# A transformer block on one core: the first row tiles' norm and projection reordered, the last tile's end in whole steps

## The chip, the cores and the metric

One Trainium2 chip, one of its cores. The metric is the device time of one execution in microseconds (us); less is better. Engines are named as in the profile: TensorE (PE; its weight loads are PEld), VectorE (DVE), ScalarE (ACT), GpSimd (POOL), SyncE (SP). SP, ACT and POOL also issue DMA transfers, each from its own instruction stream.

## The reference, cut to what matters

A residual block on x (1 x 1024 x 1024, float32): two parallel token mixers, then a SwiGLU feed-forward, each between two RMS norms.

```
def rmsnorm(x, g):
    y = x * lax.rsqrt(jnp.mean(x * x, axis=-1, keepdims=True) + RMS_EPS)
    return y * g

h = rmsnorm(x, norm_mix_pre[l])              # (1024, 1024)
proj = h @ w_in[l]                           # columns q, k, v, f_logit, g_b, g_c, hc, two gates
logf = log_sigmoid(f_logit + b_f)            # 8 heads
m = (gated short convolution of h, with conv_w) and (forgetting attention on q, k, v, logf), merged
x = x + rmsnorm(m @ w_out[l], norm_mix_post[l])
h = rmsnorm(x, norm_ffn_pre[l])
f = (silu(h @ w_gate) * (h @ w_up)) @ w_down[l]
x = x + rmsnorm(f, norm_ffn_post[l])
```

## The kernel before, in words

Every float32 product is made as three products of split operands: a value a is written as a high half (ScalarE's rounding copy to fp32r) and a low half (VectorE's subtraction of that from a), and a*b is ah*bh + ah*bl + al*bh (`mm3`). Most projections use Strassen's seven products on 512-row blocks, so they need sums of h's blocks (hT12, hT34).

The head, which the change touches, is the first 68 us. x is cut into 8 row tiles of 128 rows (st = 0 to 7), the columns of w_in for v and f_logit (`wv`, 520 columns) into 8 parts of 128 rows (k = 0 to 7). SyncE issues, in this order: row tile 0, the norm's row (4 KB), wv parts 0 to 3, row tile 1, wv parts 4 to 7, row tile 2; the next row tiles follow as their buffers (three) come free. The norm's row is broadcast to 128 partitions by a TensorE matmul with ones (`gmp`), between 10 and 14 turns of the identity (`turns`, transposes whose results nobody reads); ScalarE later copies it to `gm`. For a row tile: ScalarE squares and sums it (`norm_sum`), VectorE and ScalarE make the scale (`rms_scale`), VectorE scales (`norm_rest`, tile hn), TensorE transposes hn in two groups of four (`turn`, tile tp), and ScalarE and VectorE split the transposed tile into halves (hB11 and hB21 for tiles 0 to 3, vf and hB22 for tiles 4 to 7). `split_wv` splits a part of wv into wvh and wvl. `v_tile` then makes v and f_logit of the row tile: for each k and each half of the columns, the three products into `pv`; the result is copied to vs, stored (POOL's queue), and the 8 f columns get the bias bf (`ff`). `rest` copies the transposed tile (tiles 0 to 3, `hraw`) or makes Strassen's sums (tiles 4 to 7). After the last v products (end at 68.04 us) the first two projection heads start: q's first product needs h0 and l0, made early, and k's needs h and l, which ScalarE and VectorE make of a weight tile that waits for the head's memory.

A planner orders instructions per engine by program order and its own time estimates; `strict[0]` names engines whose instructions keep the program's order (`keep_in_program_order`), all engines in the first part of the head. Each engine's instructions run in order; so an instruction that waits holds all behind it.

The end: the feed-forward's down projection makes the last four row tiles' last column half (`product` with `last_parts`): per row tile (sl) 21 products of late operands into one accumulator; then ScalarE squares and sums it, the scale is made, VectorE applies scale and residual (`finish`), SyncE stores. Of the last row tile the last 12 products run as two column halves of 256 (`HALVES`), the square and the multiplication by the norm's row follow each half.

Of the kernel before, what the change touches and what calls it, by code (L numbers as in the profile page):

```python
# [46 lines left out]
def block_kernel(  # L47
# [121 lines left out]
    nc.gpsimd.dma_start(bf, b_f[0].partition_broadcast(P))  # L169

# [72 lines left out]
    xq.append(load_x(1))  # L243
    for _ in range(4):
        load_wv()
# [6 lines left out]
    gm = ax.tile([P, D], F32, name="gm")  # L252


    spin = psa.tile([P, 4, P], F32, tag="mm", name="spin")
    gmp = psa.tile([P, 2, NC], F32, tag="pv", name="gmp", bufs=2)

    def turns(n):
        for _ in range(n):
            nc.tensor.transpose(spin[:, 0, :], ident, ident)  # L260
# [23 lines left out]
    def norm_rest(st, xt, hn, rs):  # L284

        for n in range(2) if st == 0 else (None,):
            c = slice(0, D) if n is None else (n1, n2)[n]
            nc.vector.scalar_tensor_tensor(
                hn[:, c], xt[:, c], rs, gm[:, c] if n is None else gmp[:, n, :],
                op0=ALU.mult, op1=ALU.mult,  # L290
            )
        if st + 3 < ST:
            xq.append(load_x(st + 3))
        return hn
# [5 lines left out]
    hraw = None  # L300

    def turn(st, hn):

        nonlocal hraw
        sl = st % 4
        ss = slice(sl * P, (sl + 1) * P)
        tps = []
        for q in range(2):
            tp = psa.tile([P, 4, P], F32, tag="mm", name="tp")
            for k in range(4):  # L310
                kt = 4 * q + k
                nc.tensor.transpose(tp[:, k, :], hn[:, kt * P : (kt + 1) * P], ident)
            tps.append(tp)
        if st < 4:
            if hraw is None:
                hraw = ah.tile([P, KT, NC], F32, name="hraw")
            ops = []
            for q, hb_ in enumerate((hB11, hB21)):
                hh, hl = (t[:, :, ss] for t in hb_)
                if st == 0:  # L320
                    copy(hh, tps[q])
                    split_wv(q + 2, "h")
                    sub(hl, tps[q], f32(hh))
                    split_wv(q + 2, "l")
                else:
                    split(hh, hl, tps[q])
                ops.append((hh, hl))

            def rest():
                for q in range(2):  # L330
                    copy(hraw[:, 4 * q : 4 * q + 4, ss], tps[q])

# [27 lines left out]

    def v_tile(st, ops):
        pv = psa.tile([P, 2, NC], F32, tag="pv", name="pv", bufs=2)
# [10 lines left out]
        vs = av.tile([P, VF + 8], F32, tag="vs", name="vs", bufs=2)[:, :VF]  # L373
        copy(vs.rearrange("p (n c) -> p n c", n=2), pv[:, :, :HV])
        nc.gpsimd.dma_start(v_dram[st * P : (st + 1) * P, :], vs[:, :AW])
        add(ff[:, st, :], vs[:, AW:VF], bf)

    xt0, hn0, ssq0 = norm_sum(0)
    rs0 = rms_scale(ssq0)
    for k in range(2):  # L380
        split_wv(k, "h")
    norm_rest(0, xt0, hn0, rs0)
    for k in range(2):
        split_wv(k, "l")
    cur = turn(0, hn0)
    split_wv(4)
    one = norm_sum(1)
    split_wv(5)
    for n in range(2):
        copy(gm[:, n * NC : (n + 1) * NC], gmp[:, n, :])  # L390
    rs1 = rms_scale(one[2])
    split_wv(6)
    hn = norm_rest(1, *one[:2], rs1)
    split_wv(7)
    sub(mask, tri, ident)
    nc.vector.tensor_scalar(mask, mask, BIG, None, op0=ALU.mult)
    strict[0] = ("vector", "scalar")
    for st in range(ST):
# [3 lines left out]
        if st + 2 < ST:  # L402
            hn = norm(st + 2)
        if st + 3 == ST:
# [182 lines left out]
    nc.sync.dma_start(cw, conv_w[0].rearrange("t (c p) -> p t c", p=P))  # L587

# [1169 lines left out]
    def down(acc, ops, k, sl, start, stop, first, cols=slice(0, NC)):  # L1758
# [4 lines left out]
            acc[sl][:, cols], (ah[:, k, ss], al[:, k, ss]), (bh[:, k, cols], bl[:, k, cols]),  # L1763
# [3 lines left out]
    def product(acc, first, done, tail=1, between=None, parts=None):  # L1767
# [13 lines left out]
        steps_ = [(g, ops, k) for g, ops in late for k in range(min(2, NK - 2 * g))]  # L1781
# [143 lines left out]
```

## Time and profile before

| | |
|---|---|
| median of 3 runs | 1330.12 us (1329.48 to 1330.79) |
| the profiled execution | 1330.96 us, span 1329.0 us |
| TensorE matmul busy | 1315.5 us (99%), 6717 instructions |
| TensorE weight load | 1091.8 us (82%) |
| VectorE | 966.7 us (73%) |
| ScalarE | 558.0 us (42%) |
| mean granted TensorE clock | 0.999 |

How to read it: times are microseconds from the start of the span. A busy share is an average over stages with different limits; the timeline shows an instruction's start, its duration, and in brackets the idle time of its engine just before it with what ended it. "x8" is a run of eight like instructions merged to one row, whose second number is then their total. The granted clock is a share of TensorE's full speed.

### The profile page before, as it was taken

Reading aid. Unit: us, or ns where it says so; the run is one execution under the profiler, and the core shown is the slowest. Engines: PE = TensorE matmul, PEld = TensorE weight load, DVE = VectorE, ACT = ScalarE, POOL = GpSimd, SP = SyncE. Lnnn points to the kernel's source line nnn. Section 1 sums busy time; section 2 is a strip of 40 time slices with the busy share of each in tenths; the row PEclk is TensorE's granted clock in tenths of the full one; section 3 lists DMA queues with packets and bytes.
Section 4 is the critical chain, followed back from the end, with each engine's and each line's share of the span. In section 5 each row is a group of like instructions: output and inputs, shape, how many; then the busy total and the mean of one; then the engine's idle time right before and its main releaser. Section 6 shows DMA issues by size and latency. Waiting matters only on the chain.

```text
span 1329.0 us, 18042 instructions
## 1 busy us (share of the span) xinstructions
PE 1315.5 (99%) x6717; PEld 1091.8 (82%) x6717; DVE 966.7 (73%) x1532; ACT 558.0 (42%) x898; POOL 143.1 (11%) x272
## 2 busy tenths in 40 slices
PE   9999999999999999999999999999999999999997
PEld 7988888888888888888878888888888888888886
DVE  6974678765656767686699688997767776676685
ACT  6642222233345766514578332322322234444452
POOL 0011000011112212010012112121001110000000
PEclk9999999999999999999999999999999999999999
DMA  5334544455536544476166545553233328876541
GB/s 192 120 119 135 152 110 128 128 166 145 172 111 206 160 136 158 138 237 225 65 216 207 160 157 183 182 191 103 74 109 106 117 102 283 310 255 194 157 165 63
DMA packets 189097, 210.48 MB, mean 158 GB/s; under 512 B 11457, under 2 KB 137473, under 8 KB 189010
## 3 DMA queue, kind: packets, MB, share of 16 engines
q1 hardware_dynamic: 155586, 146.12, 35.5%
q0 software_dynamic: 16528, 54.84, 11.2%
q10 hardware_dynamic: 16896, 8.39, 2.1%
q8 instruction: 52, 0.85, 0.3%
q14 instruction: 35, 0.29, 0.1%
HBM read 150.78 MB, written 58.52 MB: 157 GB/s over the span
## 4 chain that ended last, share of the span: by engine, by line
PE 79%; issue 14%; DVE 2%; ACT 2%; DMA 1%; POOL 1%; DVEq 0%; SPq 0%; POOLq 0%; ACTq 0%
PE b L76 40%; PE pd L76 16%; PE pba L76 3%; PE pbb L76 3%; PE pv L76 3%; PE tps L76 3%; PE po L76 3%; PE p L76 2%; PE sp L76 2%; PE ma L76 1%; PE q L76 1%; DMA raw<-in_w_gate_up_dram 1%; PE mb L76 1%; PE tp L76 1%; POOL qk_dram L76 1%
## 5 line engine op out<-in xcount | busy, mean ns | idle before, releaser
L76 PE MATMUL b<-x,hi 128*128 128x512 f32 x1088 | 335.7, 389 | 0.1
L76 PEld LDWEIGHTS b<-x,hi 128*128 128x128 f32 x1088 | 203.9, 188 | 43.0 <-ACT c L76 0.5
L76 PE MATMUL b<-x,lo 128*128 128x512 f32 x544 | 211.8, 389 | 0.0
L76 DVE TENSOR_TENSOR c<-c,b 128x512 f32<-128x512 f32 x193 | 131.5, 682 | 58.8 <-PE b L76 51.4
L76 DVE TENSOR_TENSOR lo<-raw,hi 128x1024 fp32r<-128x1024 f32 x92 | 110.8, 1204 | 73.5 <-PE b L76 65.7
L76 ACT ACTIVATE hi<-raw 128x1024 fp32r<-128x1024 f32 (+1 forms) x99 | 100.6, 1018 | 96.8 <-PE b L76 50.3
L76 PEld LDWEIGHTS b<-x,lo 128*128 128x128 f32 x544 | 102.1, 188 | 21.4
L76 ACT ACTIVATE hi<-sx 128x1024 fp32r<-128x1024 f32 (+1 forms) x43 | 44.8, 1043 | 147.4 <-PE b L76 140.5
L76 ACT ACTIVATE sgf<-c 128x512 f32<-128x512 f32 x31 | 19.6, 633 | 133.2 <-DVE c L76 114.0
L76 DVE TENSOR_TENSOR lo<-sx,hi 128x1024 fp32r<-128x1024 f32 (+1 forms) x43 | 51.5, 1198 | 27.9 <-PE b L76 26.7
L76 DVE TENSOR_TENSOR sx<-raw 128x512 f32<-128x512 f32 x78 | 53.6, 687 | 19.9 <-DMA raw<-in_w_in_dram 10.4
L76 PE MATMUL pd<-hi,lo 128*128 128x512 f32 (+1 forms) x163 | 62.8, 385 | 0.0
L76 PE MATMUL pd<-hi 128*128 128x512 f32 (+1 forms) x163 | 62.4, 386 | 0.0
L76 PE MATMUL pd<-ghi 128*128 128x512 f32 (+1 forms) x149 | 57.9, 389 | 1.1 <-DVE um L76 1.1
L76 PE MATMUL pd<-glo,ghi 128*128 128x512 f32 (+1 forms) x149 | 57.8, 388 | 0.0
L76 PE MATMUL pd<-ghi,glo 128*128 128x512 f32 (+1 forms) x149 | 57.8, 388 | 0.0
L76 PE MATMUL b<-hT34h,hi 128*128 128x512 f32 x136 | 53.2, 391 | 0.8 <-DVE c L76 0.8
L76 PE MATMUL b<-hT34h,lo 128*128 128x512 f32 x136 | 52.9, 389 | 0.0
L76 PE MATMUL b<-hT34l,hi 128*128 128x512 f32 x136 | 52.9, 389 | 0.0
L76 PE MATMUL b<-hT12h,hi 128*128 128x512 f32 x136 | 52.9, 389 | 0.0
L76 PE MATMUL b<-hT12l,hi 128*128 128x512 f32 x136 | 52.9, 389 | 0.0
L76 PE MATMUL b<-hT12h,lo 128*128 128x512 f32 x136 | 52.9, 389 | 0.0
(427 smaller groups left out, 3050.3 us busy)
## 6 DMA issues: line engine op xcount, KB each, us to landing
raw<-in_w_gate_up_dram SPq DMA_DIRECT2D x55, 512.0 KB, 3.8
raw<-in_w_in_dram SPq DMA_DIRECT2D x35, 512.0 KB, 4.9
a_dramS<-um POOLq DMA_DIRECT2D x44, 256.0 KB, 3.2
a_dramA<-um POOLq DMA_DIRECT2D x33, 256.0 KB, 2.7
sg<-sg_dram SPq DMA_DIRECT2D x32, 256.0 KB, 4.0
x<-wo_dram SPq DMA_DIRECT2D x16, 512.0 KB, 7.4
graw<-a_dramS SPq DMA_DIRECT2D x14, 512.0 KB, 3.6
sg_dram<-c POOLq DMA_DIRECT2D x24, 256.0 KB, 3.6
```

The lines of the kernel that those rows point to most:

```text
L76: ins = getattr(self.engine, name)(*args, **kw)
```

## The change

Head: the norm row is loaded to 128 partitions by a DMA on ScalarE's queue (`gm`), no matmul, no copy; all 26 turns run ahead. wv's odd parts are issued by ScalarE, the even ones by SyncE. `rms_scale` is cut in two functions, hn of tiles 0 and 1 is scaled in two halves. wv's high halves 0 to 2 are made ahead of tile 0's copies, the others behind tile 1's square; low halves 3 to 7 follow tile 1's norm. The products of tiles 0 and 1 are no longer `mm3` per k but sorted: high-high, low-high and high-low apart, with the last high-low ones (k = 6, 7 of tile 0, 4 to 7 of tile 1) behind tile 2's transposes. All engines keep program order up to there. bf, the mask and conv_w are loaded or made later. End: the last row tile takes the same whole steps as the others.

```
@@ head
-    nc.gpsimd.dma_start(bf, b_f[0].partition_broadcast(P))
...
     def rms_scale(ssq, rest=None, tile_=st_tile, w=1):
-        va, sq, r0 = (tile_(n, w) for n in ("va", "sq", "r0"))
+        return rms_finish(*rms_root(ssq, rest, tile_, w), tile_, w)
+
+    def rms_root(ssq, rest=None, tile_=st_tile, w=1):
+        va, sq = (tile_(n, w) for n in ("va", "sq"))
...
+        return va, sq
+
+    def rms_finish(va, sq, tile_=st_tile, w=1):
+        r0 = tile_("r0", w)
         nc.vector.reciprocal(r0, sq)
...
-    def load_wv():
+    def load_wv(engine):
...
-        nc.sync.dma_start(wr, win[k * P : (k + 1) * P, C_V : C_V + VF])
+        engine.dma_start(wr, win[k * P : (k + 1) * P, C_V : C_V + VF])
...
+    gm = ax.tile([P, D], F32, name="gm")
     xq = deque([load_x(0)])
-    grow = ap.tile([P, D], F32, tag="hn", name="grow", bufs=2)[0:1, :]
-    nc.sync.dma_start(grow, norm_mix_pre)
-    for _ in range(4):
-        load_wv()
+    nc.scalar.dma_start(gm, norm_mix_pre[0].partition_broadcast(P))
+    for k in range(3):
+        load_wv((nc.sync, nc.scalar)[k % 2])
     xq.append(load_x(1))
-    for _ in range(4):
-        load_wv()
+    for k in range(3, KT):
+        load_wv((nc.sync, nc.scalar)[k % 2])
     xq.append(load_x(2))
     warm = st_tile("warm")
     nc.scalar.activation(warm, ones[:, 0:1], AF.Sqrt)
...
-    turns(10)
-    for n in range(2):
-        nc.tensor.matmul(
-            gmp[:, n, :], ones[0:1, :], grow[:, n * NC : (n + 1) * NC], start=True, stop=True
-        )
-    turns(14)
+    for _ in range(26):
+        nc.tensor.transpose(spin[:, 0, :], ident, ident)
...
-        for n in range(2) if st == 0 else (None,):
...
+        for c in (n1, n2) if st < 2 else (slice(0, D),):
             nc.vector.scalar_tensor_tensor(
...
+                hn[:, c], xt[:, c], rs, gm[:, c], op0=ALU.mult, op1=ALU.mult
...
+    def turned(hn, q):
+        tp = psa.tile([P, 4, P], F32, tag="mm", name="tp")
+        for k in range(4):
+            kt = 4 * q + k
+            nc.tensor.transpose(tp[:, k, :], hn[:, kt * P : (kt + 1) * P], ident)
+        return tp
+
+    def upper(st, tps):
+        ss = slice(st * P, (st + 1) * P)
+        ops = [tuple(t[:, :, ss] for t in b) for b in (hB11, hB21)]
+        def rest():
+            for q in range(2):
+                copy(hraw[:, 4 * q : 4 * q + 4, ss], tps[q])
+        return ops, rest
...
+    PASSES = dict(hh=(0, wvh), lh=(1, wvh), hl=(0, wvl))
...
+    def v_mm(pv, ops, k, which, start=False, stop=False):
+        half, w = PASSES[which]
+        for n in range(2):
+            nc.tensor.matmul(
+                pv[:, n, :HV], ops[k // 4][half][:, k % 4, :], w[:, k, n, :],
+                start=start, stop=stop,
+            )
+
+    def v_out(st, pv):
+        vs = av.tile([P, VF + 8], F32, tag="vs", name="vs", bufs=2)[:, :VF]
+        copy(vs.rearrange("p (n c) -> p n c", n=2), pv[:, :, :HV])
+        nc.gpsimd.dma_start(v_dram[st * P : (st + 1) * P, :], vs[:, :AW])
+        return lambda: add(ff[:, st, :], vs[:, AW:VF], bf)
...
+    def high(op, tp):
+        copy(op[0], tp)
+
+    def low(op, tp):
+        sub(op[1], tp, f32(op[0]))
+
+    one = norm_sum(0)
+    rs0 = rms_scale(one[2])
+    for k in range(3):
         split_wv(k, "h")
+    hn0 = norm_rest(0, *one[:2], rs0)
+    split_wv(0, "l")
+    tp0 = [turned(hn0, q) for q in range(2)]
+    op0, rest0 = upper(0, tp0)
+    high(op0[0], tp0[0])
+    low(op0[0], tp0[0])
+    high(op0[1], tp0[1])
+    split_wv(1, "l")
+    split_wv(2, "l")
+    one = norm_sum(1)
+    root = rms_root(one[2])
+    low(op0[1], tp0[1])
+    split_wv(3, "h")
+    for k in range(4, KT):
+        split_wv(k, "h")
+    rs1 = rms_finish(*root)
+    hn1 = norm_rest(1, *one[:2], rs1)
+    pv0 = v_bank()
...
+    for k in range(3):
+        v0(k, "hh", start=k == 0)
+    v0(0, "hl")
+    for k in range(3):
+        v0(k, "lh")
+    v0(1, "hl")
+    for k in (3, 4, 5, 6):
+        v0(k, "hh")
+        v0(k, "lh")
+        if k == 3:
+            v0(2, "hl")
+    tp1 = [turned(hn1, q) for q in range(2)]
+    for which in ("hh", "lh"):
+        v0(7, which)
+    op1, rest1 = upper(1, tp1)
+    for k in (3, 4):
         split_wv(k, "l")
+        v0(k, "hl")
+    high(op1[0], tp1[0])
+    low(op1[0], tp1[0])
+    high(op1[1], tp1[1])
+    split_wv(5, "l")
+    low(op1[1], tp1[1])
+    for k in (6, 7):
+        split_wv(k, "l")
+    pv1 = v_bank()
...
+    for which in ("hh", "lh", "hl"):
+        for k in range(4):
+            v1(k, which, start=which == "hh" and k == 0)
+    v0(5, "hl")
+    for which in ("hh", "lh"):
+        for k in range(4, KT):
+            v1(k, which)
+    rest0()
+    hn = norm(2)
+    cur = turn(2, hn)
+    for k in (6, 7):
+        v0(k, "hl", stop=k == 7)
+    ff0 = v_out(0, pv0)
+    rest1()
+    for k in range(4, KT):
+        v1(k, "hl", stop=k == 7)
+    hn = norm(3)
+    ff1 = v_out(1, pv1)
+    nc.gpsimd.dma_start(bf, b_f[0].partition_broadcast(P))
     strict[0] = ("vector", "scalar")
-    for st in range(ST):
+    for st in range(2, ST):
...
+        if st == 2:
+            ff0()
+            ff1()
+            sub(mask, tri, ident)
+            nc.vector.tensor_scalar(mask, mask, BIG, None, op0=ALU.mult)
...
+        if ij == 1:
+            pinned(
+                lambda: nc.sync.dma_start(cw, conv_w[0].rearrange("t (c p) -> p t c", p=P)),
+                "sync",
+            )
@@ end, product()
-        steps_ = [(g, ops, k) for g, ops in late for k in range(min(2, NK - 2 * g))]
         for sl in range(4):
-            apart = 4 if parts and sl == 3 else 0
...
+            for g, ops in late:
+                for k in range(min(2, NK - 2 * g)):
+                    down(acc, ops, k, sl, False, 2 * g + k == NK - 1, first)
+            done(sl)
...
-    product(xb, False, last, TAIL, rows_1, last_parts)
+    product(xb, False, last, TAIL, rows_1)
```

## Rows read from the trace of the kernel before

**Rows 1.** Busy time by stage: us, each engine's busy time (instructions), granted clock, DMA share, GB/s.
```profile
0.00:68.00 68.00, 64.85 (x476) 60.44 (x477) 52.07 (x108) 43.12 (x80) 5.59 (x16) 1.00 0.49 152
68.00:1310.00 1242.00, 1239.14 (x6183) 1021.66 (x6182) 905.23 (x1398) 511.72 (x807) 137.50 (x256) 1.00 0.49 159
...
1325.00:1329.00 4.00, 0.00 (x0) 0.00 (x0) 0.90 (x2) 0.00 (x0) 0.00 (x0) 0.79 0.34 131
...
34.10:66.50 32.40, 32.40 (x275) 32.40 (x274) 30.99 (x57) 20.32 (x33) 2.72 (x5) 1.00 0.40 123
```

**Rows 2.** Chain of waits in the head: start, us, what.
```profile
8.26 3.18 PE spin L76 x14
...
56.70 11.51 PE pv L76 x96
```

**Rows 3.** Timeline of the head: start, us, engine, line, operation, idle before it.
```profile
4.54 1.06 ACT L76 ACTIVATE hn<-xt 128x1024 f32<-128x1024 f32 x1 [2.31 <-DMA xt<-in_x_dram]
...
6.79 0.16 DVE L76 TENSOR_TENSOR r<-r,t 128x1 f32<-128x1 f32 x1
...
8.30 1.41 DVE L76 SCALAR_TENSOR_TENSOR hn<-xt,r,gmp 128x512 f32<-128x512 f32 x2 [1.36 <-PE gmp L76]
...
11.23 1.91 PE L76 MATMUL tp<-ident,hn 128*128 128x128 f32 x8
...
12.98 0.47 PE L76 MATMUL pv<-wvh,hB11h 128*128 128x260 f32 x1
...
20.33 1.09 PE L76 MATMUL tp<-ident,hn 128*128 128x128 f32 x8 [0.20 <-DVE hn L76]
...
29.84 0.36 PE L76 MATMUL pv<-wvh,hB11h 128*128 128x260 f32 x1
```

**Rows 4.** Timeline of VectorE: the fifth tile's hn, the last tile's low half, l.
```profile
32.90 1.28 DVE L76 SCALAR_TENSOR_TENSOR hn<-xt,r,gm 128x1024 f32<-128x1024 f32 x1
...
59.08 0.69 DVE L76 TENSOR_TENSOR vf<-tp,vf 128x512 fp32r<-128x512 f32 x1
...
69.88 1.23 DVE L76 TENSOR_TENSOR l<-raw,h 128x1024 fp32r<-128x1024 f32 x1 [0.78 <-ACT h L76]
```

**Rows 5.** Timeline of the end: squares of the last three row tiles, what follows them.
```profile
1311.63 0.60 ACT L76 ACTIVATE junk<-pd 128x512 f32<-128x512 f32 x1 [3.68 <-PE pd L76]
...
1316.39 0.60 ACT L76 ACTIVATE junk<-pd 128x512 f32<-128x512 f32 x1 [3.75 <-PE pd L76]
...
1318.67 1.42 DVE L76 SCALAR_TENSOR_TENSOR um<-um,r,x2t 128x512 f32<-128x512 f32 x2
...
1320.97 0.39 PE L76 MATMUL pd<-ghi 128*128 128x256 f32 x1 [1.14 <-DVE um L76]
...
1322.69 0.38 ACT L76 ACTIVATE junk<-pd 128x256 f32<-128x256 f32 x1 [2.36 <-PE pd L76]
...
1324.49 1.41 DVE L76 SCALAR_TENSOR_TENSOR um<-um,r,x2t 128x512 f32<-128x512 f32 x2
```

**Rows 6.** Busy time by stage, two stretches of the head (columns as in rows 1).
```profile
4.00:6.00 2.00, 1.49 (x2) 0.83 (x3) 0.15 (x1) 1.24 (x3) 0.00 (x0) 1.00 0.72 152
8.00:10.00 2.00, 2.00 (x10) 1.81 (x10) 1.70 (x3) 0.64 (x1) 0.00 (x0) 1.00 1.03 412
```

**Rows 7.** DMA issues: transfer, queue, count, KB each, median us to landing.
```profile
gpo<-in_norm_mix_post_dram SPq DMA_DIRECT2D x1, 512.0 KB, 4.1
...
gfo<-in_norm_ffn_post_dram SPq DMA_DIRECT2D x1, 512.0 KB, 8.7
...
bf<-in_b_f_dram POOLq DMA_DIRECT2D x1, 4.0 KB, 6.3
```

**Rows 8.** Waits of SyncE's queue, 0 to 12 us: total us, times, longest.
```profile
SPq L76 <- DMA wr<-in_w_in_dram: 1.9, 3, 1.3
```

**Rows 9.** Timeline of ScalarE near 393 us: an issue, then a table load.
```profile
393.56 0.37 ACTq L76 DMA_DIRECT2D wo_dram<-l  x1
393.95 1.28 ACT L76 ACT_TABLE_LOAD   x1 [0.36 <-DVE l L76]
```

More of the change, by code (lines that the diff above doesn't have):

```diff
@@ L298, in norm @@
         return norm_rest(st, xt, hn, rms_scale(ssq))
-    hraw = None
+    hraw = ah.tile([P, KT, NC], F32, name="hraw")
+    def turned(hn, q):
[11 more added lines that the diff above has]
+        return ops, rest
     def turn(st, hn):
-        nonlocal hraw
         sl = st % 4
         ss = slice(sl * P, (sl + 1) * P)
[L307 to L313, printed above, removed]
-        if st < 4:
[L315 to L331, printed above, removed]
+        tps = [turned(hn, q) for q in range(2)]
+        if st < 4:
+            ops, rest = upper(st, tps)
+            for op, tp in zip(ops, tps):
+                split(*op, tp)
             return ops, rest
@@ L372, in v_tile @@
                 )
[L373 to L380, printed above, removed]
-        split_wv(k, "h")
-    norm_rest(0, xt0, hn0, rs0)
-    for k in range(2):
-        split_wv(k, "l")
-    cur = turn(0, hn0)
@@ L386, in block_kernel @@
[L386 to L396, printed above, removed]
+        v_out(st, pv)()
+    def high(op, tp):
[4 more added lines that the diff above has]
+    rs0 = rms_scale(one[2])
@@ new lines, in block_kernel, with v0 @@
+    pv0 = v_bank()
+    def v0(k, which, **kw):
+        v_mm(pv0, op0, k, which, **kw)
+    for k in range(3):
[14 more added lines that the diff above has]
+    for k in (3, 4):
+        split_wv(k, "l")
+        v0(k, "hl")
@@ L586, in block_kernel @@
     pairs = Pairs([(wcols(a), wcols(b)) for _, _, a, b in jobs[2:]])
-    nc.sync.dma_start(cw, conv_w[0].rearrange("t (c p) -> p t c", p=P))
     def forget_sums():
@@ L1756, in banks, with down @@
         return [bank(psm, "pd") for _ in range(4)]
-    def down(acc, ops, k, sl, start, stop, first, cols=slice(0, NC)):
+    def down(acc, ops, k, sl, start, stop, first):
         (ah, al), (bh, bl) = ops
@@ L1762, in down, with product @@
         mm3(
-            acc[sl][:, cols], (ah[:, k, ss], al[:, k, ss]), (bh[:, k, cols], bl[:, k, cols]),
+            acc[sl], (ah[:, k, ss], al[:, k, ss]), (bh[:, k, :], bl[:, k, :]),
             start, stop, **kw,
         )
-    def product(acc, first, done, tail=1, between=None, parts=None):
+    def product(acc, first, done, tail=1, between=None):
         for g in range(NG - tail):
@@ L1780, in product @@
         late = [(g, get_down()) for g in range(NG - tail, NG)]
-        steps_ = [(g, ops, k) for g, ops in late for k in range(min(2, NK - 2 * g))]
         for sl in range(4):
-            apart = 4 if parts and sl == 3 else 0
-            for g, ops, k in steps_[: len(steps_) - apart]:
-                down(acc, ops, k, sl, False, 2 * g + k == NK - 1, first)
-            if not apart:
-                done(sl)
-                continue
-            for n, cols in enumerate(HALVES):
-                for g, ops, k in steps_[-apart:]:
-                    down(acc, ops, k, sl, False, 2 * g + k == NK - 1, first, cols)
-                parts(sl, n, cols)
+            for g, ops in late:
+                for k in range(min(2, NK - 2 * g)):
+                    down(acc, ops, k, sl, False, 2 * g + k == NK - 1, first)
+            done(sl)
     def quarter(slot):
@@ L1849, in last @@
         finish(4 + sl, xts1[sl], rs, ((n2, c22[sl]), (n1, p1[sl])))
-    HALVES = slice(0, NC // 2), slice(NC // 2, NC)
-    def last_parts(sl, n, cols):
-        o, c, one = p1[sl], xb[sl], slice(sl, sl + 1)
-        junk = gp.tile([P, NC], F32, tag="junk", name="junk", bufs=2)
-        acc = sums[("c21", "both")[n]][:, one]
-        nc.scalar.activation(junk[:, cols], c[:, cols], AF.Square, accum_out=acc)
-        rest = sums["rest"][:, one]
-        if not n:
-            nc.vector.tensor_scalar(rest, acc, 1.0 / D, rest, op0=ALU.mult, op1=ALU.add)
-        else:
-            rs = rms_scale(acc, rest)
-        mul(o[:, cols], c[:, cols], gfo[:, cols])
-        if n:
-            finish(4 + sl, xts1[sl], rs, ((n2, c22[sl]), (n1, o)))
     def to(dst, how, *src):
```

14 lines of the change are left out of this document (5 added, 9 removed).

## The prediction

> **What bounds the kernel now.** I read the page's busy shares first (TensorE 99%), then busy time by stage: from 68 us to 1310 us TensorE is busy 1239.14 of 1242 us, while 3.15 us of its idle stand in the first 68 and the rest behind the last products [rows 1]. So the long middle passes on what it is given; a microsecond counts if TensorE leaves the head earlier or the end chain is shorter. The diff touches just these two places. In the chain of waits of the head, 14 idle turns of TensorE (3.18 us) stand ahead of the first transposes [rows 2]; VectorE has the first tile's norm scale at 6.95 and then waits 1.36 us for the norm row's broadcast through TensorE. The first product starts at 12.98, and from the third tile (29.84) on products come without a gap, 0.12 us each (11.51 us for 96) [rows 2, 3]. VectorE is the hidden second bound there: 30.99 of 32.40 us busy from 34.10 to 66.50 [rows 1].
>
> **The end.** Before, the last row tile's last products run as two halves; the second half waits 1.14 us for VectorE's read of the first, and the square starts at 1322.69, the final scale at 1324.49, 1.80 us later. A whole tile shows the other price: square to square of two whole tiles is 4.76 us, so the last whole square would start at 1316.39 + 4.76 = 1321.15; from square to final scale a whole tile takes 1318.67 - 1316.39 = 2.28 us, which gives 1323.43. The final scale and its stores are the same. Gain 1324.49 - 1323.43 = **1.06 us**; I see nothing that could hide it [rows 5].
>
> **The head, start of the chain.** The norm row now comes as a 512 KB transfer on ScalarE's queue beside the first row tile. Flat out the DMA engines move 412 GB/s at a busy share of 1.03, so 524 KB more, taken as interleaved with the first tile, cost 1.27 us [rows 6]: both land at 4.54 + 1.27 = 5.8 instead of 4.54. A transfer of one repeated row is shown by two rows: 4.1 us alone, 8.7 us in a crowded queue [rows 7]; I take the first, being equally early in an empty queue. ScalarE now issues five transfers before it computes. SyncE's queue shows that an issue can wait for a landing: in the head it waited three times, up to 1.3 us, for w_v parts [rows 8]. If the issues of both queues count together, ScalarE's last is about the tenth and waits for the second, the norm row (5.8). If they count apart it waits for nothing; if its turn comes later, for the first w_v part, another 1.3 us. I take the norm row. Then the issue 0.4, and the table load, which stands right behind an issue and just ahead of the first activation at the one place that shows it (1.28 us, warm 0.20) [rows 9]: the square starts at 7.7, with bounds of 5.9 (no wait) and 9.05.
> From square to scale takes 6.95 - 4.54 = 2.4 us, so hn starts at 10.2 (8.30 before). Its first half ends at 10.9, four transposes and their latency bring 11.7, copy and first product 12.3, against 12.98 before, where the transposes ran at 232 ns behind the idle turns [rows 3]: **0.7 us early**. Removing the four broadcast matmuls and, on ScalarE, the two gm copies costs nothing; hn of the second tile in halves adds 0.13 us to VectorE (1.41 for two halves against 1.28 whole) [rows 3, 4].
>
> **The head, products.** The 16 products ahead of w_v's fourth part take 1.9 us, to 14.2. On ScalarE that fourth high half stands behind the second tile's square and root: 12.3 plus a copy 0.5, square and read 1.1, the scale and root 0.6, the half itself 0.6 is 15.1. One stall of 0.9 us. From there the sorted order covers each wait: by the same durations every later operand is ready when its turn comes. So tiles 0 and 1 with tile 2's transposes end at 26.4. Before, tile 2 began at 29.84 with the fourth transposes (0.85) also done: 29.84 - 26.4 - 0.85 = **2.6 us ahead** for TensorE [rows 3].
> VectorE is not ahead. From 10.2 it has, up to the fifth hn, 18.4 us of work (four hn 5.1, sixteen low halves at 0.6 from start to start, four scales at 0.9) and 6.3 us of waits: 1.4 each for the transposes and copies of tiles 2 and 3, 1.8 while ScalarE copies an output, two raw quarters and makes a square, the rest roots and single copies. The fifth hn starts at 34.9 against 32.90, and mask and two bias adds (0.65) that were done by then still stand behind it: **2.65 us behind**. At most 1.4 of that can be won back, all the idle that VectorE had from 34.10 until its backlog ended [rows 1, 4], so it is 1.25 to 2.65 us late. The last tile's low half came at 59.08 + 0.69 = 59.77, long before TensorE began that tile at 29.84 + 38.1 - 5.7 = 62.3 (third tile's start, 288 products and four groups of transposes less one tile). Now TensorE asks for it at 62.3 - 2.6 + 0.25 = 60.0 and gets it at 61.0 to 62.4. It waits 1.0 to 2.4 us and w_v's products end 1.6 to 0.2 us earlier than before, not 2.6. The next step on the path, the second head's l, waits for ScalarE's h, which follows these products (0.78 us of idle for it before [rows 4]), and shifts by the same. I take the middle: **0.9 us** gained.
>
> **The rest at nothing.** bf moves behind the second output on POOL: issued near 30, landing 3 to 6.3 us later (6.3 as in the crowded head [rows 7]), read by VectorE at 36.1: 0 to 1.3 us in VectorE's queue, which lies within the lag's bounds. Taking it out of the head may help: the DMA rate falls to 152 GB/s in 4 to 6 us while bf is under way, and recovers to 412 [rows 6]; I count 0 because ScalarE is the later one. cw goes behind the sixth row tile on SyncE, far ahead of its reader. w_v on two queues: the parts come by about 13 us by the same rate, each ahead of ScalarE's copy of it.
>
> **Sum.** 0.9 + 1.06 = 2.0 us. The profiled execution took 1330.96 (span 1329.0), 0.84 over the median of 1330.12; I take the 2.0 from the median: **1328.1 us**. 0.2% of it is 2.66 us; that is what I hold a measurement of this kernel can tell from no change.
>
> **Rivals.** (a) VectorE is no wall: ScalarE's issues wait for nothing and the square starts at 5.9. Then every step is 1.85 earlier, VectorE's lag is -0.6 to 0.8, TensorE's lead 4.45: head gain 2.05 to 3.45, with the end 3.1 to 4.5, so 1325.6 to 1327.0. For it: nothing in the rows says that both queues share a count. Against: SyncE's waits for landings. (b) The head gains nothing: ScalarE waits for the first w_v part (1.3 us), or TensorE's products start slow. The granted clock reads 1.00 all through the head, yet transposes stood 232 ns apart after a broken start, until 13 us, and 99 ns later (8 in 1.91 us against 1.09) [rows 3], half speed, so the 1.2 GHz level. The new order has 26 turns, some 6 us, and then idles some 3 us until 10.9: whether the level rises in the turns and stays is shown by no row. Five us at half speed are 2.5 us of products, of which the 0.9 stall is covered and VectorE's lag covers more: 0.7 to 1.4 lost. Either makes the head -0.5 to +0.6: 1329.2 to 1330.0 with the longer end counted.
> The Trainium skill (TensorE: Matmul & The Clock Gate, Part 1) says that the default is the throttled clock and idleness brings it back, which speaks for (b); the granted share falls to 0.79 in the run's last 4 us, with TensorE idle, which agrees [rows 1]. By that rule the time would be about 1329.5.
> (c) Slower: the norm row does not come like a plain load but like the 8.7 us row [rows 7]. It lands at 9.4, or 10.7 with the first tile beside it; ScalarE, in order behind its last issue, makes the square at 11.3 to 12.6, 3.6 to 4.9 us later than forecast. The head loses 2.7 to 4.0, the end returns 1.06: 1331.7 to 1333.1. It decides from a landing at about 8 us on (head gain gone), and beyond 10.6 it shows as over 0.2%.
>
> **Chances.** Forecast 0.40 (its own range 1327.4 to 1328.9), (a) 0.28, (b) 0.24, (c) 0.08. Faster by over 0.2% (under 1327.46) is (a) and a little of the forecast, 0.31; slower by over 0.2% is most of (c) and unseen mishaps, 0.08; the rest 0.61. The range leaves out the outer half of (a) and (c): 1325.8 to 1330.6.
>
> **What would show it.** The last square near 1321.15 minus the head's gain, no wait of TensorE for um there; ScalarE's table load behind its issues and the square near 7.7; first product near 12.3; one TensorE wait near 14 to 15 on wvh; VectorE's low half of the last tile later than TensorE wants it; l of the first projection at 69 to 70. The forecast is wrong if the square starts under 7 or over 9, if the first products are 0.23 us apart, or if VectorE ends its backlog before 66.5.

## The result, and the profile after

The changed kernel is slower: 1333.84 us by the median of 16 runs (1332.49 to 1335.71), against 1330.43 us for the kernel before on the same chip, a ratio of 1.0025 with a 95% interval of 1.0017 to 1.0033. The forecast was 1328.1, its range ended at 1330.6. The profiled execution took 1333.32 us with a span of 1331.5; before it was 1330.96 and 1329.0. The two traces are compared by their spans, 2.5 us apart.

Busy time by stage comes first (columns as in [rows 1]: length, then busy time of PE, PEld, DVE, ACT, POOL, the granted clock, DMA share, GB/s).

```profile
0.00:68.00 68.00, 59.03 (x460) 57.89 (x461) 47.80 (x104) 40.61 (x76) 5.58 (x16) 0.95 0.43 142
68.00:1310.00 1242.00, 1237.74 (x6183) 1020.41 (x6182) 907.10 (x1396) 513.32 (x806) 137.50 (x256) 1.00 0.50 160
...
11.10:17.90 6.80, 5.09 (x23) 4.88 (x24) 5.93 (x16) 5.01 (x11) 0.00 (x0) 0.50 0.64 221
```

The loss is in the head. TensorE is busy 59.03 of its first 68 us, against 64.85 [rows 1], and the granted clock has a hole: 0.50, the 1.2 GHz level, from 11.10 to 17.90. Why TensorE starts late is read from the chain of waits of the first 16 us (start, us, what):

```profile
1.19 6.50 DMA wr<-in_w_in_dram
...
7.72 0.33 ACTq L76
...
8.08 1.28 ACT L76
...
9.38 0.20 ACT warm L76
9.58 1.05 ACT hn L76 x2
...
11.91 0.76 DVE hn L76
```

The chain goes through the landing of w_v's first part (7.69) into an issue of ScalarE (7.72). Behind that issue stand the table load, warm and the first square. ScalarE's timeline shows the same, with its earlier issues:

```profile
0.74 0.41 ACTq L76 DMA_DIRECT2D gm<-in_norm_mix_pre_dram  x1
1.18 0.94 ACTq L76 DMA_DIRECT2D wr<-in_w_in_dram  x2
6.21 1.84 ACTq L76 DMA_DIRECT2D vf<-in_w_in_dram  x2
8.08 1.28 ACT L76 ACT_TABLE_LOAD   x1 [8.08 <-DMA wr<-in_w_in_dram]
...
9.49 1.04 ACT L76 ACTIVATE hn<-xt 128x1024 f32<-128x1024 f32 x1
```

SyncE's sixth issue stands between ScalarE's third and fourth:

```profile
6.00 0.33 SPq L76 DMA_DIRECT2D vf<-in_w_in_dram  x1
```

ScalarE's first three issues go out in the first 2.2 us. The fourth goes at 6.21, when the norm row has landed (6.19), the fifth at 7.72, when w_v's first part has landed. Counted over both queues, eight issues go out without a wait; the ninth (SyncE's, which waits for the first row tile), the tenth and the eleventh each follow a landing. The square starts at 9.49 against 4.54 [rows 3]. The Trainium skill (DMA: Bandwidth & Descriptors, Anatomy of one DMA — SWDGE (gpsimd) path) says that any semaphore wait happens on the issuing sequencer, before dispatch. The trace agrees: it is ScalarE that stands still, for 4.1 us up to 6.21.

TensorE's rows of the head answer to those of [rows 3]:

```profile
12.81 1.94 PE L76 MATMUL tp<-ident,hn 128*128 128x128 f32 x8 [6.94 <-DVE hn L76]
14.59 1.67 PE L76 MATMUL pv<-wvh,hB11h 128*128 128x260 f32 x6
...
64.02 0.28 PE L76 MATMUL pv<-wvh,vf 128*128 128x260 f32 x1
...
74.03 0.50 PE L76 MATMUL b<-hB11h,l 128*128 128x512 f32 x1 [0.72 <-DVE l L76]
```

The turns end at 5.88, TensorE is idle for 6.94 us, and the first eight transposes take 1.94 us instead of 1.09, at half clock. The first product starts at 14.59, 1.6 us later than before. Up to the first projection product (69.78 against 68.04) this hardly changes: 55.2 us of TensorE's time, 55.1 before. Then the fifteenth product of the projection, the first that needs the l made at 72.76 (below), waits 0.72 us and starts at 74.03; before it was at 71.24. So 1.6 (start) + 0.1 (the v products) + 1.1 (l) = 2.8 us late when the head is over. VectorE's rows say why l is late (answering to [rows 3, 4]):

```profile
11.91 1.41 DVE L76 SCALAR_TENSOR_TENSOR hn<-xt,r,gm 128x512 f32<-128x512 f32 x2
...
28.54 0.69 DVE L76 TENSOR_TENSOR hB11l<-tp,hB11h 128x512 fp32r<-128x512 f32 x1 [1.45 <-ACT hB11h L76]
...
31.52 0.15 DVE L76 TENSOR_SCALAR va<-ssq 128x1 f32<-128x1 f32 x1 [1.70 <-ACT hn L76]
...
35.51 0.69 DVE L76 TENSOR_TENSOR hB11l<-tp,hB11h 128x512 fp32r<-128x512 f32 x1 [1.44 <-ACT hB11h L76]
...
39.00 1.29 DVE L76 SCALAR_TENSOR_TENSOR hn<-xt,r,gm 128x1024 f32<-128x1024 f32 x1
...
60.56 0.68 DVE L76 TENSOR_TENSOR vf<-tp,vf 128x512 fp32r<-128x512 f32 x1
...
71.61 1.23 DVE L76 TENSOR_TENSOR hT34l<-t,hT34h 128x1024 fp32r<-128x1024 f32 x1 [0.28 <-ACT hT34h L76]
72.76 1.22 DVE L76 TENSOR_TENSOR l<-raw,h 128x1024 fp32r<-128x1024 f32 x1
```

The fifth hn comes at 39.00 against 32.90 [rows 4]. VectorE then has hardly any idle time to catch up in: its backlog ends at 72.8, and l follows it at once. Before, VectorE's backlog ended at 66.5, and it stood idle for 2.45 us ahead of the last bias add and for 0.78 us ahead of l (69.88 [rows 4]):

```profile
68.93 0.17 DVE L76 TENSOR_TENSOR ff<-vs,bf 128x8 f32<-128x8 f32 x1 [2.45 <-ACT vs L76]
```

The lag of some 6 us uses up these 3.2, and l still comes 2.9 us later. The last tile's low half, on the other hand, is made from 60.56 to 61.24 us, and TensorE begins that tile at 64.02: it did not wait there. The end came as worked out (answering to [rows 5]):

```profile
1319.93 0.60 ACT L76 ACTIVATE junk<-pd 128x512 f32<-128x512 f32 x1 [3.75 <-PE pd L76]
...
1324.69 0.60 ACT L76 ACTIVATE junk<-pd 128x512 f32<-128x512 f32 x1 [3.74 <-PE pd L76]
...
1326.97 1.42 DVE L76 SCALAR_TENSOR_TENSOR um<-um,r,x2t 128x512 f32<-128x512 f32 x2
```

Square to square is 4.76 us, square to final scale 2.28, and the wait of TensorE for um is gone. TensorE was 3.5 us behind before its last row tile; the final scale is 2.48 behind (1326.97 - 1324.49): the end returned 1.06.

### The profile page after: what moved, and what is told of

It reads as the page before. It is cut to its first block, busy times and chain, and to the rows that moved or that the text cites. A ratio compares the mean times of both kernels' runs of the same rounds, so it can differ in the third digit from the quotient of the medians.

```text
span 1331.5 us, 17999 instructions
## 1 busy us (share of the span) xinstructions
PE 1311.4 (98%) x6703; PEld 1090.1 (82%) x6703; DVE 966.2 (73%) x1531; ACT 557.9 (42%) x894; POOL 143.1 (11%) x272
## 4 chain that ended last, share of the span: by engine, by line
PE 77%; issue 14%; DVE 3%; ACT 3%; DMA 2%; POOL 1%; DVEq 0%; ACTq 0%; SPq 0%; POOLq 0%
PE b L76 40%; PE pd L76 16%; PE pba L76 3%; PE pbb L76 3%; PE po L76 3%; PE tps L76 3%; PE p L76 2%; PE pv L76 2%; PE sp L76 2%; PE ma L76 1%; PE q L76 1%; PE tp L76 1%; DMA raw<-in_w_gate_up_dram 1%; PE mb L76 1%; POOL qk_dram L76 1%
## 5 line engine op out<-in xcount | busy, mean ns | idle before, releaser
L76 DVE TENSOR_TENSOR sx<-raw 128x512 f32<-128x512 f32 x78 | 53.6, 687 | 17.9 <-DMA raw<-in_w_in_dram 9.2
L76 PE MATMUL pd<-hi,lo 128*128 128x512 f32 x160 | 62.2, 389 | 0.0
L76 PE MATMUL pd<-hi 128*128 128x512 f32 x160 | 61.9, 390 | 0.0
L76 PE MATMUL pd<-ghi 128*128 128x512 f32 x148 | 57.6, 389 | 0.0
L76 PE MATMUL pd<-glo,ghi 128*128 128x512 f32 x148 | 57.6, 389 | 0.0
L76 PE MATMUL pd<-ghi,glo 128*128 128x512 f32 x148 | 57.6, 389 | 0.0
```

The lines of the kernel that those rows point to most:

```text
L76: ins = getattr(self.engine, name)(*args, **kw)
```

## The experiments

Theory A: ScalarE's late start makes the loss; its issues of w_v wait for landings and hold the first square. Theory B: the new order itself makes it; VectorE comes late whatever the loads do. Theory C: the half clock makes it. Each run is compared with the kernel before, run beside it on the same chip; "before" stands for its median there. In the diffs the lines are of the kernel named.

**The end alone.** The kernel before, last row tile in whole steps:

```
-            apart = 4 if parts and sl == 3 else 0
+            apart = 0
```

> The kernel before with the last row tile's steps whole, nothing else changed. The whole price of the end was worked out as 1.06 us, and the changed kernel's last square to final scale shows it (2.28 us, no wait for um). All theories: 1.06 us less than before, 1329.4 against 1330.4; last square 2.0 us earlier than 1322.69. If the end's gain is an accident of one trace, no difference.

Measured: 1329.87 us, before 1331.0, ratio 0.9991 (0.9983 to 1.0000). The span fell by 1.1 us (1327.9), and the final scale comes 2.28 us behind the last square. The square itself came 1.6 us earlier (1321.11), as the prediction's 1321.15 had it; the expected 2.0 was wrong. The gain is about the 1.06 of the forecast, at the edge of what can be measured.

**SyncE issues all of w_v.** The changed kernel, ScalarE left with one issue, the norm row's:

```
-        load_wv((nc.sync, nc.scalar)[k % 2])
+        load_wv(nc.sync)
```

> The changed kernel, but all eight w_v parts are issued by SyncE; ScalarE issues the norm row alone. Theory A (ScalarE's in-order issues are the cause): its last issue waits for nothing, the table load is over by 3 us, the first square starts when the row tile lands, near 6.0 instead of 9.49, and the 3.5 us come back nearly whole: 1330.0 to 1331.0, VectorE's fifth hn near 35.5 instead of 39.0. Theory B (the sorted, strict order makes VectorE late whatever the start): VectorE's fifth hn stays behind 37 and the time is 1332 or more. If the granted clock does not fall because TensorE's pause is shorter, another 1 us less.

Measured: 1330.60, before 1331.0, ratio 0.9998 (0.9989 to 1.0006). Relative to before that is 3.8 us less than the changed kernel. ScalarE's timeline:

```profile
0.74 0.40 ACTq L76 DMA_DIRECT2D gm<-in_norm_mix_pre_dram  x1
1.17 1.28 ACT L76 ACT_TABLE_LOAD   x1 [1.17 <-PEq L1955]
...
6.22 1.06 ACT L76 ACTIVATE hn<-xt 128x1024 f32<-128x1024 f32 x1 [3.56 <-DMA xt<-in_x_dram]
```

The table load now stands in the time in which ScalarE waits for data anyway, and the square starts when the first row tile has landed. That is theory A, with 3.3 us of square and 3.8 us of time. The granted clock fell here too (0.50 from 9.5 to 12.9 us), after a pause of TensorE of 2.81 us. Theory A is not the whole: with the end's 1.1 in it this version should be clearly faster than before, and it is only level.

**Turns until the first transposes.** The changed kernel:

```
-    for _ in range(26):
+    for _ in range(75):
```

> The changed kernel with 75 turns instead of 26, so that TensorE is busy until about the first transposes (12.8). Theory C (the clock's fall at 11.1, after a pause from 5.9 on, costs): the granted clock stays at full from its rise on, the first eight transposes take 1.1 instead of 1.94 us, products stand 0.12 us apart from the first, and 1.5 to 2.5 us come back: 1331.3 to 1332.3. Theory A: ScalarE and VectorE set the pace, the transposes' 0.8 us are all that comes back: 1333.0. If the turns delay the transposes, slower than 1333.8.

Measured: 1332.58, before 1331.0, ratio 1.0014 (1.0005 to 1.0023). One stretch, columns as above:

```profile
9.00:11.00 2.00, 2.00 (x21) 2.00 (x20) 0.15 (x1) 1.77 (x5) 0.00 (x0) 1.00 1.02 404
```

TensorE is never idle and the clock stays full; the first transposes take 1.23 us, the projection starts at 68.75 instead of 69.78, and the time lies between the two expectations. The clock is worth 1.0 us there. By the medians it is 1.8, but the interval overlaps that of the changed kernel (1.0017 to 1.0033), so that figure is not clear of noise. It is a part of the loss and not the loss.

**The new order with the old loads.** The changed kernel, but all loads, the broadcast by TensorE and the 10 and 14 turns as before; the late bf and the whole end stay:

```
-    nc.scalar.dma_start(gm, norm_mix_pre[0].partition_broadcast(P))
...
+    grow = ap.tile([P, D], F32, tag="hn", name="grow", bufs=2)[0:1, :]
+    nc.sync.dma_start(grow, norm_mix_pre)
...
+    turns(10)
+    for n in range(2):
+        nc.tensor.matmul(
+            gmp[:, n, :], ones[0:1, :], grow[:, n * NC : (n + 1) * NC], start=True, stop=True
+        )
+    turns(14)
```

> The changed kernel's order of work, but with the loads of before: all on SyncE, the norm row of 4 KB broadcast by TensorE between 10 and 14 turns, copied to gm by ScalarE behind the second tile's root; bf still late, the end whole. Theory A (loads and issues are the cause): no later than the kernel before with a whole end, 1328.0 to 1329.4. Theory B (the order itself makes VectorE late): VectorE's fifth hn 2 us or more behind that of before (32.90) and the time 1330.5 to 1332.

Measured: 1332.19, before 1331.0, ratio 1.0011 (1.0002 to 1.0020). Here ScalarE starts as before (square 4.56, hn at 8.43, first product 13.04), and yet the fifth hn comes at 37.78. VectorE's waits are the same three as in the changed kernel:

```profile
27.32 0.69 DVE L76 TENSOR_TENSOR hB11l<-tp,hB11h 128x512 fp32r<-128x512 f32 x1 [1.44 <-ACT hB11h L76]
...
30.31 0.15 DVE L76 TENSOR_SCALAR va<-ssq 128x1 f32<-128x1 f32 x1 [1.70 <-ACT hn L76]
...
34.30 0.69 DVE L76 TENSOR_TENSOR hB11l<-tp,hB11h 128x512 fp32r<-128x512 f32 x1 [1.44 <-ACT hB11h L76]
...
37.78 1.29 DVE L76 SCALAR_TENSOR_TENSOR hn<-xt,r,gm 128x1024 f32<-128x1024 f32 x1
```

So theory B holds too. The order costs by itself: 1.2 us, or 2.3 without the end's 1.1.

**The new loads with the old order.** The kernel before with the norm row by DMA on ScalarE's queue, w_v on two queues and 26 turns; order, early bf and halved end as before.

```
-    nc.sync.dma_start(grow, norm_mix_pre)
...
+    nc.scalar.dma_start(gm, norm_mix_pre[0].partition_broadcast(P))
+    for k in range(3):
+        load_wv((nc.sync, nc.scalar)[k % 2])
```

> The kernel before with the changed kernel's loads only: norm row by DMA on ScalarE, w_v on two queues, 26 turns ahead; order of work, bf and halved end as before. Theory A (late square from ScalarE's issues): the square near 9.5, hn near 11.9, 3.6 us late, the granted clock falls in TensorE's pause, and the kernel is 2 to 3.5 us slower than before: 1333 to 1334.5. Theory B: the old order catches up in VectorE's idle time (2.45 us ahead of the last bias add): 0.5 to 1.5 us slower.

Measured: 1333.48, before 1330.44, ratio 1.0021 (1.0012 to 1.0030). The loads alone cost 3.0 us. Order (2.3) and loads (3.0) less the end (1.1) would make 4.2, the change made 3.4. The intervals, about 1.2 us either way, do not tell the two apart; as both delay the same VectorE, a full sum was not to be expected. The square is at 10.53 here, 1.0 later than in the changed kernel; the early bf is the one transfer that differs up to there (last section).

**The fourth tile's norm moved ahead.** In the new order the norm of the fourth tile stands behind everything that ScalarE does for the third: copies of the transposes, an output, two raw quarters. Put right behind the third tile's norm:

```
-    hn = norm(2)
-    cur = turn(2, hn)
+    hn2 = norm(2)
+    hn = norm(3)
+    cur = turn(2, hn2)
...
-    hn = norm(3)
     ff1 = v_out(1, pv1)
```

> The changed kernel with one step moved: the fourth row tile's norm (square, root, scaling) right behind the third's, ahead of the third's transposes, as the kernel before has the two squares side by side. Theory B, sharpened: ScalarE's fixed order puts each square behind the copies of the tile before, so from the third tile on a tile's norm is a chain of 6 to 7 us and VectorE idles in it. Then the fourth hn follows the third by 2 instead of 7 us, the fifth hn starts near 35.5 instead of 39.0, l near 70 instead of 72.75, and the time falls by 2 to 3 us to about 1331. Rival: the chain is not what delays l (the late start is): less than 0.7 us.

Measured: 1331.46, before 1330.44, ratio 1.0007 (0.9998 to 1.0016), 2.4 us better than the changed kernel relative to before. VectorE's hn of the third to fifth tile:

```profile
25.62 1.28 DVE L76 SCALAR_TENSOR_TENSOR hn<-xt,r,gm 128x1024 f32<-128x1024 f32 x1
...
28.08 1.29 DVE L76 SCALAR_TENSOR_TENSOR hn<-xt,r,gm 128x1024 f32<-128x1024 f32 x1
...
34.77 1.28 DVE L76 SCALAR_TENSOR_TENSOR hn<-xt,r,gm 128x1024 f32<-128x1024 f32 x1
```

The fourth hn comes 2.5 us behind the third instead of 7.0, the fifth at 34.77 instead of 39.00, and TensorE no longer waits for l (first projection product 68.66, fifteenth 71.86, 3.2 us apart as before).

**Both undone.** The changed kernel with the two edits above:

```
-        load_wv((nc.sync, nc.scalar)[k % 2])
+        load_wv(nc.sync)
...
-    hn = norm(2)
-    cur = turn(2, hn)
+    hn2 = norm(2)
+    hn = norm(3)
+    cur = turn(2, hn2)
...
-    hn = norm(3)
```

> The same move in the kernel whose w_v parts are all issued by SyncE. Theory B: both causes gone, fifth hn near 32, l near 66.5, and 1328.0 to 1329.0, under the kernel before with the whole end (1329.9). Rival: TensorE then has no more to win (its products end near 65.9 already) or the gain is lost behind the head as with the SyncE issues alone: 1330 to 1330.6.

Measured: 1328.25, before 1330.44, ratio 0.9981 (0.9972 to 0.9989): faster than before. 3.8 and 2.4 would make 6.2 us, together they made 5.6.

**Fewer turns before.** The kernel before with the whole end and four turns behind the broadcast:

```
-    turns(14)
+    turns(4)
```

> The kernel before with the whole end and 4 instead of 14 turns behind the norm row's broadcast. If those turns hold the first transposes back, they start near 9.2 instead of 11.3 and the first product near 11.2; VectorE has 2.45 us of idle to give, so 0.8 to 1.7 us less than the whole end alone: 1328.2 to 1329.1. Rival: the clock rises later for it, the products run at half speed for longer, and nothing or less than nothing is gained: 1329.9 or more.

Measured: 1327.48, before 1330.44, ratio 0.9976 (0.9966 to 0.9986). TensorE's timeline:

```profile
8.24 1.11 PE L76 MATMUL spin<-ident 128*128 128x128 f32 x4
9.24 1.94 PE L76 MATMUL tp<-ident,hn 128*128 128x128 f32 x8
11.01 0.58 PE L76 MATMUL pv<-wvh,hB11h 128*128 128x260 f32 x1
```

The 14 turns, which the chain of waits had shown ahead of the first transposes [rows 2], held them back by 2 us: without ten of them the first product starts at 11.01 instead of 12.98, though the transposes take 1.94 us, as long as at half clock in the changed kernel (the granted clock reads 1.00 here). Less the end's 1.1 that is 1.8 us, a little more than expected and twice what the forecast had for the whole head.

**The table load ahead of the issues.** The changed kernel with `warm` moved up:

```
+    warm = st_tile("warm")
+    nc.scalar.activation(warm, ones[:, 0:1], AF.Sqrt)
     xq = deque([load_x(0)])
     nc.scalar.dma_start(gm, norm_mix_pre[0].partition_broadcast(P))
...
-    warm = st_tile("warm")
-    nc.scalar.activation(warm, ones[:, 0:1], AF.Sqrt)
```

> The changed kernel with ScalarE's table load and its warming activation put ahead of ScalarE's five transfers, not behind them. Theory (the issues that wait for landings hold ScalarE, and the table load of 1.28 us and warm of 0.2 us stand behind them): the last issue still goes at about 7.7 us, the square follows it at once, at 8.1 to 8.3 instead of 9.48, first product near 13.2, and the run is 1.0 to 1.4 us shorter than the changed kernel, 1332.4 to 1332.8 by its median of 1333.8 (ratio to before 1.0015). Against it: the norm row is issued 1.5 us later (2.2 instead of 0.74), so if its landing moves with that (7.0 to 7.7 instead of 6.2) the issues wait longer, the square comes at 8.8 to 9.5, and nothing is won. Rival (the square waits for the landing of the first row tile or of the norm row, not for the issues): no gain either, but then the square starts right at a landing.

Measured: 1331.15, before 1330.41, ratio 1.0004 (0.9995 to 1.0013): 2.7 us better relative to before, twice what was expected. The chain of waits:

```profile
1.04 5.49 DMA gm<-in_norm_mix_pre_dram
...
6.55 0.33 ACTq L76
...
6.93 1.16 ACT hn L76 x2
```

Two things changed. The table load (1.5 us with warm) is out of the chain, and ScalarE's last issue waited for another landing: the norm row's, at 6.53, and not w_v's first part at 7.69. The first row tile landed at 4.18, and ScalarE's fourth issue followed at 4.20, ahead of SyncE's sixth (7.72); so ScalarE's last was the tenth of both queues and not the eleventh. The norm row was issued at 1.04, beside the table load, not at 2.2 as feared. The square came 2.6 us earlier, 1.4 by the one and 1.2 by the other. Which landing an issue waits for hangs on the order of all issues, and a small shift changes it.

**More turns in the version with both undone.**

```
-    for _ in range(26):
+    for _ in range(45):
```

> The version without ScalarE's issues of w_v and with the fourth tile's norm moved ahead (1328.25 us), with 45 idle turns instead of 26, so that TensorE does not stand idle from 6.5 us until the first transposes at 9.34. If the pause is what brings the half-speed clock (8.94 to 12.36 there): the granted clock stays at 1.00 through the head, eight transposes take 1.1 us instead of 1.94, the first product starts at 10.5 to 10.8 instead of 11.11, the first b product 0.3 to 1.0 us earlier, 1327.3 to 1328.0 in all. If VectorE alone sets the head's end, the products are quicker but first b stays at 64.8 and the time at 1328.2. Too many turns would hold the transposes back: then they start later than 9.4 and the gain is gone.

Measured: 1326.78, before 1330.41, ratio 0.9972 (0.9962 to 0.9983); its interval overlaps that of the version with 26 turns, so a gain is not shown. The clock did not stay full, against the expectation:

```profile
9.00:11.00 2.00, 1.49 (x10) 1.10 (x11) 1.83 (x4) 1.16 (x3) 0.00 (x0) 1.00 1.05 407
11.30:14.60 3.30, 3.30 (x17) 3.30 (x16) 3.16 (x10) 2.90 (x7) 0.00 (x0) 0.50 1.04 412
```

The first product came 0.4 us earlier (10.74) and the second tile's hn 0.45 (14.03 against 14.48), the first projection product did not (65.03 against 64.85). The half clock lasted as long as with 26 turns (3.4 us), only later, over products. So the second tile's transposes start at 16.45 against 16.22, and VectorE waits for them, 1.04 us where it had waited 0.37:

```profile
17.71 0.69 DVE L76 TENSOR_TENSOR hB11l<-tp,hB11h 128x512 fp32r<-128x512 f32 x1 [1.04 <-ACT hB11h L76]
```

The half clock took back what the turns had won; what a full clock is worth in this version the run does not show.

**bf behind the third row tile**, in the kernel before with whole end and 4 turns:

```
-    nc.gpsimd.dma_start(bf, b_f[0].partition_broadcast(P))
...
     xq.append(load_x(2))
+    nc.sync.dma_start(bf, b_f[0].partition_broadcast(P))
```

> The kernel before with whole steps at the end and 4 idle turns behind the broadcast (1327.48 us), with bf issued by SyncE behind the third row tile instead of by GpSimd at the start. Theory (bf's 128 small packets disturb the first loads: the kernel before with the new loads and bf early makes its first square at 10.52, the changed kernel with bf late at 9.48): the first row tile lands 0.3 to 1.0 us earlier than 4.5, hn0 and first b come earlier by as much, 1326.5 to 1327.2. Rival (that 1.0 us has another cause): first square at 4.5 as before, 1327.3 to 1327.6. bf is read at about 19 us and lands by 14, so nothing should wait for it.

Measured: 1327.08, before 1330.41, ratio 0.9977 (0.9968 to 0.9986), no measurable difference from early bf (0.9976). In the trace the head is 0.44 us earlier (square 4.25 against 4.52, first projection product 65.62 against 66.06), at the lower end of what was expected. The profile shows bf as 32 packets, not 128.

**The best of these.** The version with both undone, and the table load ahead of ScalarE's one issue:

```
+    warm = st_tile("warm")
+    nc.scalar.activation(warm, ones[:, 0:1], AF.Sqrt)
     xq = deque([load_x(0)])
     nc.scalar.dma_start(gm, norm_mix_pre[0].partition_broadcast(P))
...
-    warm = st_tile("warm")
-    nc.scalar.activation(warm, ones[:, 0:1], AF.Sqrt)
```

> The version with w_v issued by SyncE alone, the fourth tile's norm moved ahead and 26 idle turns (1328.25 us), with ScalarE's table load and warming activation ahead of its one issue, the norm row's. Theory: as in the run that moved them in the changed kernel, the norm row is issued 0.3 us later, so the first row tile lands at 4.2 (before with the row beside it: 6.0) and the row at about 6.5. The square starts at 4.2 to 4.3, the scale is ready at 6.65, hn0 starts at 6.6 to 6.8 instead of 8.44, the first product near 9.1 instead of 11.1. VectorE and the chain of norms then start 1.8 us earlier; if nothing else holds them, first b at 63.1 and 1326.4 us. Rival (the parts of w_v become the wall, as they land no earlier than before, about 0.7 us apart from 7.7 on): hn0 is early, but first products and low halves wait for w_v's parts, the fifth hn comes at 29.8 to 30.9 instead of 29.1, and the time is 1327.2 to 1328.3.

Measured: 1326.74, before 1331.18, ratio 0.9967 (0.9955 to 0.9979), 4.4 us under the kernel before. It is the lowest ratio here, but its interval overlaps those of the versions with 45 and with 4 turns. ScalarE's and TensorE's timelines:

```profile
0.74 1.28 ACT L76 ACT_TABLE_LOAD   x1 [0.74 <-PEq L1955]
1.04 0.42 ACTq L76 DMA_DIRECT2D gm<-in_norm_mix_pre_dram  x1
...
4.44 1.06 ACT L76 ACTIVATE hn<-xt 128x1024 f32<-128x1024 f32 x1 [2.21 <-DMA xt<-in_x_dram]
```

```profile
7.78 1.23 PE L76 MATMUL tp<-ident,hn 128*128 128x128 f32 x8 [1.84 <-DVE hn L76]
9.86 0.98 PE L76 MATMUL pv<-wvh,hB11h 128*128 128x260 f32 x6 [0.85 <-ACT hB11h L76]
```

The norm row is issued 0.3 us later than the first row tile, and the tile lands at 4.4 instead of 6.0. hn starts at 6.88. A little of that is lost to w_v's parts, as the rival had it: the first copy of one waits 1.19 us for its landing, VectorE waits for ScalarE behind it, and the fifth hn comes at 29.59, between the two expectations (29.1 and 29.8 to 30.9).

## Why the prediction was wrong

The step that failed is the start of the chain, "I take the norm row": it put the first square at 7.7. The issues of both queues do count together, but ScalarE's last was the eleventh and not "about the tenth", so it waited for the third landing, w_v's first part, at 7.69. With issue, table load and warm that makes 9.49, beyond the upper bound of 9.05, since that part had been expected at 7.1. That is 1.8 us on every step behind it. The mechanism had been seen, the wrong landing was chosen. Taking all of w_v's issues off ScalarE brought the square 3.3 us forward and gave 3.8 us.

Second, the clock. The forecast kept its price for rival (b) and cost it at nothing in the likeliest case, while its own timeline had TensorE idle for some 3 us until 10.9. The pause became 6.94 us, and the level fell at 11.1. Transposes and first products ran at 1.2 GHz until 17.9. The Trainium skill (TensorE: Matmul & The Clock Gate, Part 1) says that idleness brings the throttled clock back; the trace agrees. By that rule the forecast would have been about 1329.5, still too low; by the run with 75 turns the price is 1.0 us at the first projection product.

Third, VectorE's delay. That VectorE comes late and that TensorE waits for l was right. The wait from which the 0.9 us was worked out was not: the forecast had TensorE wait 1.0 to 2.4 us for the last tile's low half, but that was ready 2.8 us before TensorE began the tile (61.24 and 64.02). The lag stayed in the sums that VectorE makes behind it and reached TensorE only at l, which the forecast had left to ScalarE's h.

The size was wrong too: "2.65 us behind" at the fifth hn became 6.1. Of the 4.1 us that hn came after the forecast's 34.9, 1.7 are the late start (11.91 against 10.2). The half clock added 1.1: with 75 turns VectorE took 26.0 us from the first hn to the fifth, here 27.1. Further on the forecast had listed the waits one by one (1.4 and 1.8, they measured 1.45, 1.44 and 1.70), but left out that ScalarE makes the sixth tile's square ahead of the fifth's root, so VectorE waits 0.9 more. The last 0.4 are not accounted for. Moving one norm won 2.4 us: the order was costly by itself, and that was a term that the sum hid in a lag it took as partly free.

Fourth, the rivals. (b) priced a w_v wait and a slow clock as alternatives ("either makes the head -0.5 to +0.6"), and its sum does not come out: with the end's 1.06 that head gives 1328.5 to 1329.6, not 1329.2 to 1330.0. The two came together, and the late square made the slow clock worse: with the square at 6.22 the clock fell as well, but for 3.4 us after a pause of 2.8, here for 6.8 after 6.9. (a) had a square at 5.9 win 3.1 to 4.5 us; the run with SyncE's issues, square at 6.22, won 0.4, so an early start alone does not make the new order pay. The rival on the slower side, (c), named a late landing of the norm row; the row landed at 6.19, like a plain load, and the late start came through the issues instead. Its structure, ScalarE in order behind its last issue, was right, its cause not. And the range, up to 1330.6, left out all of (c), which began at 1331.7, not its outer half.

What held: the end (1.06 forecast, about 1.1 measured, alone and in place); the landing of the norm row and the first tile at 5.8 (6.2 and 6.0); TensorE's gain by sorted products, in part. With the clock full (75 turns) TensorE needs 54.6 us from the first v product to the first projection product, 0.5 less than before, where the forecast had 1.9 for the order of the products.

What stays open: the 2.8 us at the head's end grew to 3.5 by 757 us. Followed product by product against the kernel before, the changed kernel loses 1.8 us between the first projection product and 765 us, the l wait included, and the version with SyncE's issues 3.5 (its fifteenth product is still 1.0 us ahead, 70.24 against 71.24). The best version loses 1.2, the one with 45 turns nothing. Those with the old order lie between 0.5 us gained and 0.1 lost. The steps stand at the l wait, near 87, 214 and 272 us, and from 681 to 757 us, where TensorE waits for single operands, up to 1.3 us longer; some go the other way. Each figure is of one execution, and the run with the end alone, whose head is that of before, has a step of 0.6 us itself (near 214). The order of TensorE's instructions there is nearly the same in all versions; what makes the waits longer behind most of the new heads was not tried.

## What to carry to other kernels

An engine that computes should not issue transfers ahead of its first work unless they are few: one that waits for a landing holds everything behind it, and which landing that is changes with the order of all issues. When a start moves, ask at once what idles meanwhile; a cold clock is priced on top of the delay, not instead of it. Before reordering a head, take away what visibly stands on its chain: ten idle turns less won 1.8 us, where the rearrangement as made lost; repaired by three more edits it won 3.3 (4.4 less the end's 1.1).

## What the hardware showed that was not expected

A transfer of 4 KB can hold back 512 KB loads. With the new loads and bf issued early (old order), the rate from 6 to 8 us falls to 132 GB/s:

```profile
6.00:8.00 2.00, 0.00 (x0) 0.00 (x0) 0.00 (x0) 0.00 (x0) 0.00 (x0) 1.00 0.78 132
```

In the changed kernel, where bf comes late, it is 369:

```profile
6.00:8.00 2.00, 0.00 (x0) 0.00 (x0) 0.00 (x0) 0.00 (x0) 0.00 (x0) 1.00 1.03 369
```

With the old loads and bf behind the third row tile, the rate from 4 to 6 us is 232, against 152 with bf early [rows 6]; the run's time did not show the difference:

```profile
4.00:6.00 2.00, 1.88 (x3) 0.87 (x4) 0.30 (x2) 1.35 (x3) 0.00 (x0) 1.00 1.04 232
```

w_v's first part landed at 8.73 in the first of these three and at 7.69 in the second.

Two transfers issued at the same moment on two queues finish together and late (6.0 and 6.2 us). With the second issued 0.3 us later the first is done at 4.2 to 4.4, and the second at 6.5 (the changed kernel with the table load ahead): the first won 1.6 to 1.8 us, the second lost 0.3.

The granted clock fell after a pause of 2.85 us (26 turns, both undone: half speed from 8.94) and did not after one of 1.84 us (the best version: 1.00 from 4.5 to 20 us, eight transposes in 1.23). But with 45 turns and a pause of 1.40 us it fell at 11.26, with TensorE at work. So no length of pause is shown to be safe. Nor is the clock the same in each execution: the kernel before and the run with the end alone have one program up to there, and their first eight transposes took 1.91 [rows 3] and 1.24 us, while the granted clock reads 1.00 in both.
